# Two LayerNorms of a transformer block: half of the feature tiles turned by DMA instead of TensorE, and the stages behind them started with feature pairs by token halves

## The chip, the cores and the metric

The kernel runs on one core of a Trainium2 chip. Its engines are TensorE (PE; its weight loads have a row of their own, PEld), VectorE (DVE), ScalarE (ACT), GpSimd (POOL) and SyncE (SP, which issues nearly all DMAs). Each engine executes its own list of instructions in order, and engines wait for each other by semaphores. The metric is the device time of one execution in microseconds (us): 2433.39 us, the median of three runs (2433.3 to 2434.96).

## The reference

One layer of a streaming encoder on 256 tokens of 2048 features, all in float32:

```python
h = LN(alpha*h + 0.5*SwiGLU_1(h))                       # ffn1 and its LayerNorm
mix = W_out[ sig(g_A)*(A(h) W_oA) + sig(g_B)*(B(h) W_oB) ]
h = LN(alpha*h + mix)                                   # A: chunked attention, B: latent attention
h = LN(alpha*h + CrossAttn(h, LN(mem)))                 # cross attention and its LayerNorm
h = LN(alpha*h + 0.5*SwiGLU_2(h))                       # ffn2
# layer_norm(x, g, b): (x - mean) * rsqrt(var + eps) * g + b over the 2048 features
```

The change concerns the first and the third LayerNorm, and the products that come first behind each: the values of attention A (`h @ w_in`, 1024 of its columns) behind the first, and the first 512 gate and 512 up columns of ffn2 behind the third.

## The kernel before, in words

The stream `h` lies by tokens: two tiles `h0`, `h1` of 128 tokens x 2048 features (token halves, `tt` 0 and 1). A product needs it turned, features on the partitions: sixteen feature tiles `kt` of 128, four to a quarter, in blocks T0 to T3 (one block is one quarter, both token halves). Every operand is held as a high and a low part whose sum is the float32 value: ScalarE casts the high part, VectorE subtracts it for the low part. A product is then three matmuls: weight high with both parts of the stream, weight low with its high part. The stream is the stationary operand and 512 weight columns move.

**The two LayerNorms before the change.** The stage ahead ends with an output column whose products are computed for token half 0 first, then for half 1 (`skewed`, L813), from four weight pieces that are kept for both. So the statistics of half 0 are ready while TensorE works on half 1. `ln_steps` (L436) gives three steps for a half: `ln_scale` (mean and reciprocal root by a dozen small VectorE instructions), `ln_T` of quarters 0 and 1, and `ln_T` of quarters 2 and 3. `ln_T` (L406) scales a quarter (VectorE for even ones, L413; ScalarE for odd ones, L415), turns its four tiles on TensorE (L421), applies gain and bias from PSUM (two tiles on ScalarE, L428; two on VectorE, L430), and splits the result into its parts (L255, L256).

**The stages behind them before.** They are skewed too: four pieces of four feature tiles for half 0, 48 matmuls for all sixteen tiles and 512 columns, then the same four pieces for half 1, then four pieces of the next 512 columns for both halves. The steps of half 1's LayerNorm are woven in at 0, 3 and 4 items.

**Turning by DMA.** Elsewhere (the mixer's LayerNorm in `turned_norm`, L1386, the hidden units, the queries) a tile is turned without TensorE: ScalarE separates the two 16-bit halves of each float32 into planes (`planes`, L845/L846), SyncE issues a DMA that transposes 16-bit elements (`send`, L849/L850), and ScalarE joins the planes again (`join`, L852/L854). In `turned_norm` gain and bias follow (two tiles on ScalarE, L1426; two on VectorE, L1428), and the split.

**What sets the order.** `run` (L179) walks a list of items. It loads weight pieces ahead into three raw buffers (L193, 1 MB each), and splits them into two unit buffers `hi`/`lo` or into blocks that are free then. SyncE's list has the weight loads and the turning DMAs in one row; a load is put behind the last turning DMA (`issue_after(self.sent.ins)`, L192). Inside that, a tile scheduler orders the instructions of each engine once, when the program is built.

## Time and profile before

| | |
|---|---|
| median of three runs | 2433.39 us |
| profiled execution | 2432.52 us |
| its span, first to last instruction | 2430.7 us |
| PE busy | 2422.3 us (100%) |
| DVE busy | 2130.9 us (88%) |
| ACT busy | 1553.2 us (64%) |
| DMA, mean rate | 212 GB/s |
| chain that ended last | PE 89%, DVE 4%, ACT 3%, DMA 1% |

A busy engine executes an instruction; waiting doesn't count, but matmuls are pipelined and the end of one is modelled, so a short wait of TensorE can be hidden in its busy row. The row of its weight loads (PEld) is the sharper one: each matmul here has its own weight load, and their start times give TensorE's pace. The chain is followed back from the last instruction, at each step to what released it.

### The profile page before, as it was taken

Reading aid. Unit: us, or ns where it says so; the run is one execution under the profiler, and the core shown is the slowest. Engines: PE = TensorE matmul, PEld = TensorE weight load, DVE = VectorE, ACT = ScalarE, POOL = GpSimd, SP = SyncE. Lnnn points to the kernel's source line nnn. Section 1 sums busy time; section 2 is a strip of 40 time slices with the busy share of each in tenths; the row PEclk is TensorE's granted clock in tenths of the full one; section 3 lists DMA queues with packets and bytes.
Section 4 is the critical chain, followed back from the end, with each engine's and each line's share of the span. In section 5 each row is a group of like instructions: output and inputs, shape, how many; then the busy total and the mean of one; then the engine's idle time right before and its main releaser. Section 6 shows DMA issues by size and latency. Waiting matters only on the chain.

```text
span 2430.7 us, 29702 instructions
## 1 busy us (share of the span) xinstructions
PE 2422.3 (100%) x11280; PEld 2022.8 (83%) x11280; DVE 2130.9 (88%) x2437; ACT 1553.2 (64%) x2022; POOL 35.9 (1%) x81
## 2 busy tenths in 40 slices
PE   9999999999999999999999999999999999999999
PEld 8888888888888888888888888888888888888887
DVE  8999989899889998779788889979879999888997
ACT  6676745666555557878565687765666675556662
POOL 0000000000000001000000000000000000000000
PEclk9999999999999999999999999999999999999999
DMA  7766656667656657776577577655556766666665
GB/s 268 252 212 214 207 200 222 210 201 219 224 176 215 216 195 248 229 210 176 183 246 256 167 241 213 220 181 192 190 199 214 229 221 210 220 207 207 200 220 182
DMA packets 176414, 516.20 MB, mean 212 GB/s; under 512 B 111728, under 2 KB 112496, under 8 KB 121104
## 3 DMA queue, kind: packets, MB, share of 16 engines
q1 hardware_dynamic: 170816, 495.83, 61.6%
q0 software_dynamic: 4592, 17.30, 2.2%
q8 instruction: 88, 1.44, 0.2%
q10 hardware_dynamic: 864, 1.18, 0.1%
q14 instruction: 54, 0.44, 0.1%
HBM read 485.30 MB, written 2.10 MB: 201 GB/s over the span
## 4 chain that ended last, share of the span: by engine, by line
PE 89%; DVE 4%; ACT 3%; DMA 1%; issue 1%; SPq 0%; DVEq 0%; ACTq 0%
PE at L311 24%; PE mm L311 23%; PE at L366 11%; PE mm L366 11%; PE mm L298 10%; PE mm L277 4%; PE mm L279 2%; DVE lo L267 2%; ACT hi L264 1%; PE at L1034 1%; PE at L1505 0%; PE at L277 0%; DMA raw<-w_xv 0%; PE at L1088 0%; ACT H L854 0%
## 5 line engine op out<-in xcount | busy, mean ns | idle before, releaser
L264 ACT CAST hi<-raw 128x1024 fp32r<-128x1024 f32 (+1 forms) x852 | 804.0, 981 | 458.0 <-PE at L311 150.1
L267 DVE TENSOR_TENSOR lo<-raw,hi 128x2048 fp32r<-128x2048 f32 (+1 forms) x427 | 902.0, 2114 | 134.8 <-ACT hi L264 129.0
L311 PE MATMUL mm<-hi,T 128*128 128x512 f32 (+1 forms) x1312 | 307.5, 384 | 0.8 <-DVE v L400 0.7
L311 PEld LDWEIGHTS mm<-hi,T 128*128 128x128 f32 x1312 | 244.5, 188 | 46.9 <-DVE v L400 1.1
L264 ACT CAST X<-H 128x1024 fp32r<-128x1024 f32 (+1 forms) x170 | 174.8, 1035 | 160.9 <-DVE H L248 119.9
L311 PE MATMUL at<-hi,T 128*128 128x512 f32 x1136 | 272.3, 390 | 0.0
L311 PEld LDWEIGHTS at<-hi,T 128*128 128x128 f32 x1136 | 213.3, 188 | 44.5
L267 DVE TENSOR_TENSOR X<-H,X 128x2048 fp32r<-128x2048 f32 (+1 forms) x85 | 191.4, 2252 | 64.7 <-ACT X L264 64.7
L311 PE MATMUL mm<-lo,T 128*128 128x512 f32 (+1 forms) x656 | 158.4, 383 | 0.0
L311 PE MATMUL at<-lo,T 128*128 128x512 f32 x568 | 141.0, 389 | 0.0
L311 PEld LDWEIGHTS mm<-lo,T 128*128 128x128 f32 x656 | 122.3, 188 | 22.4
L311 PE MATMUL at<-hi,H 128*128 128x512 f32 x560 | 133.8, 390 | 0.0
L311 PEld LDWEIGHTS at<-lo,T 128*128 128x128 f32 x568 | 106.7, 188 | 22.1
L311 PEld LDWEIGHTS at<-hi,H 128*128 128x128 f32 x560 | 105.0, 188 | 21.5
L250 DVE TENSOR_TENSOR H<-H,raw 128x512 f32<-128x512 f32 (+1 forms) x170 | 115.4, 679 | 2.2
L311 PE MATMUL mm<-hi,H 128*128 128x512 f32 x480 | 115.5, 392 | 0.1
L311 PEld LDWEIGHTS mm<-hi,H 128*128 128x128 f32 x480 | 89.6, 188 | 18.9 <-DVE w L684 0.5
L248 DVE TENSOR_TENSOR H<-raw 128x1024 f32<-128x1024 f32 (+1 forms) x85 | 102.1, 1201 | 0.6 <-DMA raw<-w_gate 0.4
L366 PE MATMUL mm<-X,X 128*128 128x512 f32 x342 | 91.4, 393 | 0.0
L264 ACT CAST X<-raw 128x1024 fp32r<-128x1024 f32 (+1 forms) x54 | 55.4, 1035 | 47.9 <-DVE raw L250 38.6
L366 PE MATMUL at<-X,X 128*128 128x512 f32 (+1 forms) x315 | 82.6, 386 | 0.7 <-ACT X L264 0.7
L854 ACT COPY w<-w 128x1024 uint16<-128x1024 uint16 (+1 forms) x60 | 75.7, 1275 | 1.4 <-DMA w<-w 1.4
(387 smaller groups left out, 4151.3 us busy)
## 6 DMA issues: line engine op xcount, KB each, us to landing
raw<-ffn_w_in SPq DMA_DIRECT2D x150, 1024.0 KB, 4.9
raw<-ffn_w_out SPq DMA_DIRECT2D x66, 1024.0 KB, 4.9
raw<-w_gate SPq DMA_DIRECT2D x32, 1024.0 KB, 4.8
raw<-ffn_w_out_r SPq DMA_DIRECT2D x16, 1024.0 KB, 4.9
raw<-w_qk SPq DMA_DIRECT2D x16, 1024.0 KB, 5.6
raw<-w_o_b SPq DMA_DIRECT2D x16, 1024.0 KB, 4.8
raw<-w_out SPq DMA_DIRECT2D x16, 1024.0 KB, 5.0
raw<-w_xk SPq DMA_DIRECT2D x16, 1024.0 KB, 5.4
```

Of the source, the lines that this page charges most:

```text
L248: self.nc.vector.tensor_tensor(two[0], two[1], raw[:, :m].unsqueeze(1).to_broadcast([P, 2, m]), ALU.add)
L250: self.nc.vector.tensor_tensor(t[:, a * m:a * m + m], t[:, b * m:b * m + m], raw[:, a * m:a * m + m], ALU.add)
L264: self.last_hi = self.nc.scalar.copy(hi[:, c:d], src[:, c:d])
L267: self.last_lo = self.nc.vector.tensor_tensor(lo[:, :n], src, hi[:, :n].bitcast(F32), ALU.subtract)
L277: self.nc.tensor.matmul(ps, hi[j], x.both(kt), start=(j == 0), stop=False)
L279: self.last_mm = self.nc.tensor.matmul(ps[:, :S], lo[j], x.at(0, kt), start=False, stop=(j == n - 1))
L298: self.last_mm = self.nc.tensor.matmul(ps, x.at(xi, kt)[:, tt * P:(tt + 1) * P], w[wi][:, j * 512 + c:j * 512 + c + m], start=(start and j ...
L311: self.last_mm = self.nc.tensor.matmul(ps[tt, g][:, :n], x.at(xi, kt)[:, tt * P:(tt + 1) * P], w[wi][:, c:c + n], start=first and j + wi + ...
L366: self.last_mm = self.nc.tensor.matmul(bank[:, :m], a[xi], v[wi][:, c * m:(c + 1) * m], start=own and first and wi + xi == 0, stop=own and ...
L854: self.nc.scalar.copy(self.words(u, n).rearrange("p (c k) -> p k c", k=2), self.words(s, n).rearrange("p (k c) -> p k c", k=2))
L1034: nc.tensor.matmul(ps[:, c0:c0 + nk], q[:, tt * P:(tt + 1) * P], k[:, :nk], start=(j == 0), stop=(j == len(parts) - 1))
```

## The change

For the LayerNorms behind ffn1 and behind the cross attention, quarters 0 and 1 are still turned on TensorE (`near`, which calls `ln_T`). Quarters 2 and 3 take the way over DMA: `planes`, `send`, `join`, gain and bias, split, with blocks `F` and `X2` for the planes. All of quarters 2 and 3 is scaled on VectorE. These steps have priority 0, where the others keep the raised one.

The stage behind starts with `skewed_pairs`: a weight piece is now two feature tiles of two column groups (1024 columns). The first four pieces (feature tiles 0 to 7, quarters 0 and 1) run for token half 0, then again for half 1; the last four (tiles 8 to 15) for both halves at once. The number of matmuls and the bytes of weights are the same. Arrays of weights are laid out anew for that, before the kernel runs. Some PSUM tiles change banks (`n % 2 ^ 1` in the gates).

```diff
-                self.add(f, prio=prio, held=main[i][2] if i < len(main) else 0)
+                f, p = f if isinstance(f, tuple) else (f, prio)
+                self.add(f, prio=p, held=main[i][2] if i < len(main) else 0)
...
-    def mm_pair(self, ps, w, n, x, kts, first, last):
+    def mm_pair(self, ps, w, n, x, kts, first, last, tts=(0, 1)):
 
         for wi in range(2):
             for j, kt in enumerate(kts):
-                for tt in range(2):
+                for tt in tts:
...
-        first = self.collect(lambda: self.skewed(
-            part, (), (None, None, ("X0", "X1", "early"), ("H4", "H5"))))
-        self.weave(first, dict(zip((0, 3, 4), before)))
...
+        side = dict(before)
+        for i, c in enumerate(SUMS_IN):
+            side.setdefault(9 + i, []).append((self.forms_step(fx, SUMS_IN, c, xT), 0))
+        self.skewed_pairs(self.t[tag + "_w_in"][0], ps, xT, side, (None, None, ("X0", "X1", "early"), ("H4", "H5")))
...
+    def skewed_pairs(self, src, ps, xT, side, tags):
+
+        kept = {}
+
+        def add(k, tts, tags=None, held=0, keep=False, again=False):
+            def fn(w=None):
+                if keep:
+                    kept[k] = w
+                w = kept.pop(k) if again else w
+                if k == 0:
+                    ps.update({(tt, g): self.group_tile(0) for tt in tts for g in range(2)})
+                self.mm_pair(ps, w, 512, xT(), (2 * k, 2 * k + 1), k == 0, k == 7, tts)
+            self.add(fn, *(() if again else ((src[:, k * 2048:(k + 1) * 2048], tags),)), held=held)
+
+        def build():
+            self.skewed(lambda tt, k, **kw: add(k, (tt,), **kw), (), tags)
+            for k in range(4, 8):
+                add(k, (0, 1))
+        self.weave(self.collect(build), side)
...
+        va, ps, gates, fx = {}, {}, {}, {}
+
+        def values():
+            va["t"] = self.block("H4", (P, 2, 1024))
+            for n in range(2):
+                for tt in range(2):
+                    (nc.vector.tensor_copy if tt else nc.scalar.copy)(
+                        va["t"][:, tt, n * 512:(n + 1) * 512], ps[tt, n])
+        side = dict(steps(1))
+        for i, c in enumerate(SUMS_GATE):
+            side.setdefault(9 + i, []).append((self.forms_step(fx, SUMS_GATE, c, xT), 0))
+        side[12].insert(0, values)
+        self.skewed_pairs(t["w_va"][0], ps, xT, side, (None, None, ("H5", "H0", "early"), ("X0", "X1", "turned")))
...
-            self.pair_group(n % 2, t["w_gate"][n], 512, KT, xT, AT_GATE[n], fx, ps, qs, None, SUM_HOME + ("H5",),
+            self.pair_group(n % 2 ^ 1, t["w_gate"][n], 512, KT, xT, AT_GATE[n], fx, ps, qs, None, SUM_HOME + ("H5",),
...
-    def turned_norm(self, ln, st, x):
+    def turned_norm(self, ln, st, x, homes=("X2", "X3", "H5", "H4")):
...
+        def near(tt):
             def fn():
                 if tt == 0:
                     x["T"] = self.act(["T0", "T1", "T2", "T3"])
-                got[tt] = self.ln_scale(st[tt])
+                self.ln_T(self.h[tt], got[tt], tt, ln, x["T"], (0, 1))
...
+        if not homes[0]:
+            def low(f, *a):
+                return f(*a), 0
+            side = {0: [scale(1), low(send, 0, 2), low(planes, 0, 3)], 1: [low(send, 0, 3)], 2: [low(join, 0, 2)],
+                    3: [near(1)], 4: [low(join, 0, 3), low(planes, 1, 2)], 5: [low(send, 1, 2), low(planes, 1, 3)],
+                    6: [low(send, 1, 3)], 7: [low(join, 1, 2)], 8: [low(join, 1, 3)]}
+            return lambda tt: side if tt else ([scale(0)], [near(0)], [low(planes, 0, 2)])
...
-        ln = [self.ln_steps(n, st, x) for n in ("ln_ffn1", "ln_mix", "ln_x")]
+        ln = [self.turned_norm("ln_ffn1", st, x, (None, None, "F", "X2")), None, self.turned_norm("ln_x", st, x, (None, None, "F", "X2"))]
...
-    r["ffn2_gate"] = _tok(a["ffn2_w_in"][0][:, :512])
-    r["ffn2_up"] = _tok(a["ffn2_w_in"][0][:, D_FF:D_FF + 512])
...
-    r["w_va"] = _tok(w[:, 2 * aw:3 * aw])
+    r["w_va"] = _pairs(*_halves(w[:, 2 * aw:3 * aw]), 512, [()])
```

How this moves instructions is seen on ScalarE and SyncE. First ScalarE at the first of the two LayerNorms, before. `h_101` is token half 0, `at` is PSUM that TensorE's transposes fill, `w` holds a quarter with gain and bias, `T_768` and `T_769` are quarters 0 and 1 of the turned stream, `X_786` takes the fourth weight piece.

```order
L415 ACTIVATE h_101<-h_101,nb_5094,y_5091 128x512 x2
L428 ACTIVATE w_773_5150<-at_5145,vecs 128x128
L428 ACTIVATE w_775_5163<-at_5158,vecs 128x128
L428 ACTIVATE w_773_5150<-at_5145,vecs 128x128
L428 ACTIVATE w_775_5163<-at_5158,vecs 128x128
L255 CAST T_768_5140<-w_773_5150 128x4x128
L255 CAST T_769_5141<-w_775_5163 128x4x128
L264 CAST X_786_5224<-raw_5222 128x1024
```

The same place after. `F` and `X_782` hold the planes of quarters 2 and 3, `X_784` takes the fourth weight piece.

```order
L416 ACTIVATE h_101<-h_101,nb_5094,y_5091 128x512
L828 COPY F_5181<-h_101 128x1024
L429 ACTIVATE w_773_5150<-at_5145,vecs 128x128
L429 ACTIVATE w_775_5163<-at_5158,vecs 128x128
L429 ACTIVATE w_773_5150<-at_5145,vecs 128x128
L429 ACTIVATE w_775_5163<-at_5158,vecs 128x128
L828 COPY X_782_5200<-h_101 128x1024
L256 CAST T_768_5140<-w_773_5150 128x4x128
L256 CAST T_769_5141<-w_775_5163 128x4x128
L836 COPY F_5181<-F_5181 128x2x512
L1398 ACTIVATE F_5181<-F_5181,vecs 128x128 x2
L265 CAST X_784_5205<-raw_5203 128x1024 x2
```

Two copies into planes (L828) now stand among the activations, ahead of the casts into quarters 0 and 1, and one of the two scalings of `h_101` is gone; a join (L836) stands ahead of the casts of the fourth weight piece.

SyncE's list at the same place, before and then after. `raw_5222` and `raw_5203` are the fourth weight piece.

```order
L193 DMA raw_5047<-w_va 128x2048
L193 DMA raw_5222<-w_va 128x2048
L193 DMA raw_5345<-w_va 128x2048
L193 DMA raw_5364<-w_va 128x2048
L193 DMA raw_5422<-w_va 128x2048
```

```order
L194 DMA raw_5047<-w_va 128x2048
L832 DMA_TRANSPOSE F_5181<-F_5181 128x8x128
L194 DMA raw_5203<-w_va 128x2048
L832 DMA_TRANSPOSE X_782_5200<-X_782_5200 128x8x128
L194 DMA raw_5317<-w_va 128x2048
L832 DMA_TRANSPOSE F_5181<-F_5181 128x8x128
L194 DMA raw_5339<-w_va 128x2048
L832 DMA_TRANSPOSE X_782_5200<-X_782_5200 128x8x128
```

Each of the four turning DMAs stands ahead of a weight load: the fourth piece stands behind the first of them.

ScalarE at the second of the two LayerNorms, after. `F_14042` and `X_2167` hold the planes, `T_2153` and `T_2154` are quarters 0 and 1, `H_2169` takes the fourth weight piece.

```order
L416 ACTIVATE h_101<-h_101,nb_13951,y_13948 128x512
L828 COPY F_14042<-h_101 128x1024
L828 COPY X_2167_14061<-h_101 128x1024
L429 ACTIVATE w_2158_14008<-at_14003,vecs 128x128
L429 ACTIVATE w_2160_14021<-at_14016,vecs 128x128
L429 ACTIVATE w_2158_14008<-at_14003,vecs 128x128
L429 ACTIVATE w_2160_14021<-at_14016,vecs 128x128
L836 COPY F_14042<-F_14042 128x2x512
L256 CAST T_2153_13998<-w_2158_14008 128x4x128
L256 CAST T_2154_13999<-w_2160_14021 128x4x128
L1398 ACTIVATE F_14042<-F_14042,vecs 128x128 x2
L265 CAST H_2169_14066<-raw_14064 128x1024 x2
```

Here both copies into planes stand ahead of the activations, and the join of quarter 2 stands ahead of the casts into quarters 0 and 1.

## Rows read from the trace of the kernel before

**Rows 1.** The page: busy times, granted clock in 40 slices, one cast (mean ns).

```profile
PE 2422.3 (100%) x11280; PEld 2022.8 (83%) x11280; DVE 2130.9 (88%) x2437; ACT 1553.2 (64%) x2022; POOL 35.9 (1%) x81
...
PEclk9999999999999999999999999999999999999999
...
L264 ACT CAST X<-raw 128x1024 fp32r<-128x1024 f32 (+1 forms) x54 | 55.4, 1035 | 47.9 <-DVE raw L250 38.6
```

**Rows 2.** Waits of PEld: us in total, times, longest.

```profile
PEld mm L311 <- DVE v L400: 1.1, 1, 1.1
```

**Rows 3.** Windows: the stages behind both norms; us, busy (instructions) by engine, clock, DMA.

```profile
683.02:729.47 46.45, 46.45 (x218) 38.54 (x217) 40.15 (x73) 28.60 (x46) 1.23 (x2) 1.00 0.40 140
1741.09:1787.32 46.23, 46.23 (x218) 38.55 (x217) 34.67 (x63) 25.18 (x41) 0.00 (x0) 1.00 0.34 117
```

**Rows 4.** Timeline of PEld, first norm: start, us, instruction, idle before.

```profile
683.02 1.02 PEld L421 LDWEIGHTS at<-ident,h 128*128 128x128 f32 x8
...
684.43 1.45 PEld L298 LDWEIGHTS mm<-hi,T 128*128 128x128 f32 x7 [0.22 <-DVE T L256]
...
689.57 2.68 PEld L298 LDWEIGHTS mm<-H,T 128*128 128x128 f32 x12
692.29 1.03 PEld L421 LDWEIGHTS at<-ident,h 128*128 128x128 f32 x8
...
696.92 1.68 PEld L298 LDWEIGHTS mm<-hi,T 128*128 128x128 f32 x8
```

**Rows 5.** Timeline of PEld, second norm.

```profile
1741.09 1.02 PEld L421 LDWEIGHTS at<-ident,h 128*128 128x128 f32 x8
...
1754.78 1.68 PEld L298 LDWEIGHTS mm<-hi,T 128*128 128x128 f32 x8
```

**Rows 6.** Timeline of ACT, first norm, token half 0.

```profile
679.75 1.52 ACT L415 ACTIVATE h<-h,nb,y 128x512 f32<-128x512 f32 x2 [4.88 <-DVE nb L403]
681.17 1.73 ACT L428 ACTIVATE w<-at,vecs 128x128 f32<-128x128 f32 x4
683.03 1.14 ACT L255 CAST T<-w 128x512 fp32r<-128x512 f32 x2
```

**Rows 7.** Timeline of ACT, second norm, token half 0.

```profile
1740.20 1.14 ACT L255 CAST T<-w 128x512 fp32r<-128x512 f32 x2
```

**Rows 8.** Timeline of DVE, both norms: scalings, a low part, weights' low part.

```profile
683.68 0.69 DVE L256 TENSOR_TENSOR T<-w,T 128x512 fp32r<-128x512 f32 x1 [0.34 <-ACT T L255]
...
691.43 2.29 DVE L267 TENSOR_TENSOR X<-raw,X 128x2048 fp32r<-128x2048 f32 x1
...
1736.26 1.00 DVE L413 TENSOR_SCALAR h<-h,mv,y 128x512 f32<-128x512 f32 x2
```

**Rows 9.** Lines of the DMA way elsewhere: ns min/median/max, first and last start.

```profile
L846 ACT COPY X<-h x4: 1038/1044/1046, 1383.9 to 1390.7; 128x1024 uint16<-128x1024 uint16 x4
...
L854 ACT COPY X<-X x4: 1361/1368/1384, 1388.3 to 1407.6; 128x1024 uint16<-128x1024 uint16 x4
...
L1426 ACT ACTIVATE X<-X,vecs x8: 480/504/517, 1389.7 to 1412.9; 128x128 f32<-128x128 f32 x8
...
L1428 DVE TENSOR_SCALAR X<-X,vecs x8: 340/341/347, 1390.1 to 1410.3; 128x128 f32<-128x128 f32 x8
```

**Rows 10.** Timeline of SP: weight loads at the first norm; a turning DMA elsewhere.

```profile
666.11 8.02 SPq L193 DMA_DIRECT2D raw<-w_va  x3
...
1400.31 1.23 SPq L850 DMA_TRANSPOSE H<-H  x1
```

**Rows 11.** DMAs near 1401.5 (spaced) and 1391.3 (crowded): KB, us to landing.

```profile
raw<-w_xk SPq DMA_DIRECT2D x1, 1024.0 KB, 5.6
H<-H SPq DMA_TRANSPOSE x1, 3.1
...
raw<-w_xk SPq DMA_DIRECT2D x1, 1024.0 KB, 7.3
X<-X SPq DMA_TRANSPOSE x1, 6.1
```

More of the change, by code (lines that the diff above doesn't have):

```diff
@@ L434, in ln_T @@
                 self.ln_act = turned
-    def ln_steps(self, ln, st, x):
-        def steps(tt):
-            e = {}
-            def scale():
-                e["mr"] = self.ln_scale(st[tt])
-            def quarters(qs):
-                def fn():
-                    if tt == 0 and qs[0] == 0:
-                        x["T"] = self.act(["T0", "T1", "T2", "T3"])
-                    self.ln_T(self.h[tt], e["mr"], tt, ln, x["T"], qs)
-                return fn
-            return [scale], [quarters((0, 1))], [quarters((2, 3))]
-        return steps
     def gb_apply(self, i, h, qs=range(4)):
@@ L873, in mixer @@
         e = self.__dict__
-        va, kept, ps1 = {}, {}, {}
-        def val(n, tts, g, ps, tags=None, held=0, keep=False, again=False):
-            def fn(w=None):
-                if keep:
-                    kept[g] = w
-                w = kept.pop(g) if again else w
-                for tt in tts:
-                    if g == 0:
-                        ps[tt] = self.mm_tile()
-                    self.mm_tok(ps[tt], tt, w, xT(), range(4 * g, 4 * g + 4), g == 0, g == 3)
-                if g == 3:
-                    if "t" not in va:
-                        va["t"] = self.block("H4", (P, 2, 1024))
-                    for tt in tts:
-                        (nc.vector.tensor_copy if tt else nc.scalar.copy)(
-                            va["t"][:, tt, n * 512:(n + 1) * 512], ps[tt])
-            ap = t["w_va"][n, :, g * 2048:(g + 1) * 2048]
-            self.add(fn, *(() if again else ((ap, tags),)), held=held)
-        ps = {}
-        first = self.collect(lambda: self.skewed(
-            lambda tt, g, **kw: val(0, (tt,), g, ps, **kw), (),
-            (None, None, ("H5", "H0", "early"), ("X0", "X1", "turned"))))
-        a, b, c = steps(1)
-        self.weave(first, {0: a, 3: b, 4: c})
-        gates, fx = {}, {}
-        second = self.collect(lambda: [val(1, (0, 1), g, ps1) for g in range(4)])
-        self.weave(second, {1 + i: [self.forms_step(fx, SUMS_GATE, c, xT)] for i, c in enumerate(SUMS_GATE)}, prio=0)
+        va, ps, gates, fx = {}, {}, {}, {}
[10 more added lines that the diff above has]
+        self.skewed_pairs(t["w_va"][0], ps, xT, side, (None, None, ("H5", "H0", "early"), ("X0", "X1", "turned")))
         bias = {}
@@ L981, in lat_join @@
             return fn
-        self.pair_group(0, t["w_lat"][0], 512, KT, xT, SUMS_IN, fx, lps, lqs, None, SUM_HOME + ("H5",))
+        self.pair_group(1, t["w_lat"][0], 512, KT, xT, SUMS_IN, fx, lps, lqs, None, SUM_HOME + ("H5",))
         self.add(lat_scale, prio=SOON)
@@ L996, in kpe @@
             rope = self.rotation()
-            ps = self.at_tile()
+            ps = self.mm_tile()
             for kt in range(KT):
@@ L1393, in fn @@
             def fn():
+                if tt == 0 and homes[0]:
+                    x["T"] = self.act(["T0", "T1", "T2", "T3"])
+                got[tt] = self.ln_scale(st[tt])
+            return fn
+        def near(tt):
+            def fn():
                 if tt == 0:
                     x["T"] = self.act(["T0", "T1", "T2", "T3"])
-                got[tt] = self.ln_scale(st[tt])
+                self.ln_T(self.h[tt], got[tt], tt, ln, x["T"], (0, 1))
             return fn
@@ L1401, in fn @@
                 if tt == 0:
-                    e[q] = self.block(("X2", "X3", "H5", "H4")[q], (P, 2, 2, 512))
+                    e[q] = self.block(homes[q], (P, 2, 2, 512))
                 mean, r, nb = got[tt]
@@ L1710, in _layout @@
         r[f + "_w_in"] = _pairs(
-            w[:, D_FF:D_FF + NG * 512], w[:, :NG * 512], 512, [AT_FIRST] + [SUMS_IN] * (NG - 1))
+            w[:, D_FF:D_FF + NG * 512], w[:, :NG * 512], 512, [AT_FIRST if f == "ffn1" else ()] + [SUMS_IN] * (NG - 1))
         r[f + "_w_in_r"] = _pairs(
```

21 lines of the change are left out of this document (removed).

## The prediction

> **What bounds the kernel.** I read the page first, then TensorE's waits, the two stages in windows, and the timelines of each engine there. On the page TensorE is busy for 100% of the span at the full granted clock (2.4 GHz of its two levels) [rows 1]. The list of waits agrees: the longest single wait of its weight loads is 1.1 us, in another stage [rows 2]. So a microsecond taken from TensorE's list is gained, and a microsecond that it newly waits is lost; other engines matter only where TensorE waits for them. The two stages behind the norms take 46.45 and 46.23 us [rows 3]. Twelve matmuls take 2.72 us, from 689.57 to 692.29 [rows 4], 0.2267 each. A stage holds 192 of them, 43.5 us; what is left in the second window, 2.7 us, is 24 transposes, so 0.9 us per eight. The first window has 0.2 us more, a short wait for the low part of the turned stream at 684.43 [rows 4].
>
> **What is removed.** Each norm gives up sixteen of its 32 transposes: 4 x 0.9 = 3.6 us over both, and the 0.2 us wait. If nothing new is waited for, that is all there is to gain: 3.8 us, 0.16%.
>
> **What comes instead.** For each half, ScalarE gets two copies into planes (1.04 us each) and two joins (1.36) [rows 9] for one scaling less; VectorE gets one scaling more. Both have idle time over the whole kernel [rows 1], but here their place in the list counts. In a row of ScalarE's the next instruction starts some 0.09 us before the end of the one ahead, so I count a copy as 0.95. I follow the chain to the first matmuls of each half.
>
> *First norm, half 0.* Before, ScalarE's two scalings ran from 679.75 in 1.52 us, four activations followed, and the cast into T0 began at 683.03 [rows 6]. Now one scaling (0.72) is gone and two copies (1.9) stand ahead of that cast, 1.2 us more: cast from 684.2 to 684.8, low part 0.69 later [rows 8], 685.5. TensorE comes there at 683.02, where eight transposes were [rows 4]. Its first two matmuls use high parts, the third needs the low one, so it runs as if it had started at 685.05: 2.0 us lost.
>
> *First norm, half 1.* The fourth weight piece is now behind a turning DMA on SyncE. Before, it was loaded far ahead: three more loads of the stage go out between 666.11 and 674.1 [rows 10]. Now the first copy ends at 681.7, the turning DMA takes SyncE 1.23 us [rows 10], and the load goes at 683.0. A load behind one turning DMA landed in 5.6 us [rows 11], so 688.7. ScalarE's next instruction but for a short idle is its cast, and everything for half 1 is queued behind: two casts of the piece to 690.7 (1.04 each [rows 1]), the scaling of h1 691.4, cast of T2 692.0, join 693.3, two activations with gain and bias (0.49 each) 694.1, a wait of 0.2 for VectorE and the cast of T3 694.9, the copy of half 1 into planes 695.8, four activations 697.3, cast into T0 698.1; low part 698.8. VectorE has 2.29 us of the piece's low part [rows 8] in that time and keeps up. TensorE's own way: 685.05 + 36 matmuls 8.16 + eight transposes 0.9 + 12 matmuls 2.72 = 696.85. It needs the low part for the second matmul, so it runs as if from 698.6: 1.75 us lost. Before, this second half began at 696.92 [rows 4]: with the transposes saved up to there, the stage is 1.7 us behind.
>
> *Second norm, half 0.* VectorE scales quarters 0 and 2 from 1736.26 to 1737.26 [rows 8]; the copy of quarter 2 ends at 1738.4, that of quarter 3 at 1739.3, the activations at 1740.8. Then the join of quarter 2 stands ahead of the cast into T0, and waits for the turning DMA: 1738.4 + 3.1 [rows 11] = 1741.5, joined 1742.9, cast to 1743.5 (before, the cast began at 1740.20 [rows 7]). VectorE has a column with gain and bias (0.34 [rows 9]) and an addition to h1 (0.68) ahead of the low part: 1744.5. TensorE comes at 1741.09 [rows 5] and runs as if from 1744.05: 3.0 us lost.
>
> *Second norm, half 1.* The fourth piece is issued at 1739.65 and lands at 1745.25. Queued behind: two casts 1747.3, cast of T2 1747.9, join 1749.2, two activations 1750.0, scaling 1750.7; then ScalarE waits for VectorE, which subtracts the piece's low part until 1752.3 and applies gain and bias; cast of T3 1753.2, copy 1754.2, activations and a short wait 1755.85, cast into T0 1756.5, low part 1757.2. TensorE comes at 1744.05 + 11.8 = 1755.85 and runs as if from 1757.0: 1.1 us lost. Before, this half began at 1754.78 [rows 5], so 2.2 us behind.
>
> *Quarter 2 of half 1*, needed 52 matmuls after the start of that half, 12.0 us to the first that reads its low part. ScalarE's chain from the same start: 1.85 until the first piece's high buffer is free, two casts 1.95, copy 0.95, two casts 1.95, two joins 2.6, three activations 1.2, a cast 0.6, then the low part 0.7, in all 11.8. I count no wait, but there is no slack: a late DMA here shows in full.
>
> *The rest.* Later weight pieces are needed 5.4 us apart and cost ScalarE 2 and VectorE 2.3 of that; the changed PSUM banks keep the same number of tiles. I count them at nothing; a bound is the longest wait found now, 1.1 us, per stage.
>
> **The sum.** -3.6 - 0.2 + 2.0 + 1.75 + 3.0 + 1.1 = +4.05 us; by the starts of the second halves, 1.7 + 2.2 = 3.9. I take +4.0: 2436.5 for an execution like the profiled one (2432.52, of it 1.8 outside the span). The median of the runs lies 0.9 above that execution, so 2437.4, 0.17% slower.
>
> **Rival 1: the gain stays.** The items come in time, and the change is worth its 3.8 us: 2429.6. For it: the waits are sums of a dozen durations, and VectorE's and ScalarE's shares leave room. Against it: copies and joins stand ahead of the casts in lists that run in order, so 2.0 and 3.0 do not depend on a DMA being a little faster. Nor does a faster one help much at the second norm: half 1 is tied to the weight load, and what half 0 wins, half 1 waits.
>
> **Rival 2: loads and turning DMAs delay each other.** Where they were crowded, a turning DMA took 6.1 us and a load 7.3 [rows 11]. At 6.1 the second norm's half 0 starts 3.0 us later, and quarter 2 of half 1 comes about 3 us late at both places; the load's 1.7 us adds to half 1 at the first. In all some 9 us more, +13: 2446. It decides from a turning DMA of about 4 us, where the loss passes 0.2%. Against it: the first turning DMA of each half here goes out with no load issued in the 4 us before it, as in the spaced case.
>
> **Rival 3: the clock falls.** The row shows the full level in every slice, but no wait as long as the 3.0 us that I count [rows 1, 2]. If the clock went to its lower level (1.2 GHz) there, a matmul of 0.227 would take twice that, and 36 matmuls until the next transposes would cost 8 us: 2445. The Trainium skill (TensorE: Matmul & The Clock Gate, "Why this matters for your kernels") warns of idle gaps between bursts of matmuls, after which the clock goes back to half; by that rule the sum would be about +12, by the row alone +4. No run here shows it.
>
> **How the numbers follow.** A measurement of this kernel can tell about 0.2% (4.9 us) from no change. The chain as worked out, with a microsecond or two of error on each of five links, +1.5 to +7: 0.50, of it 0.33 within 0.2% and 0.17 slower. Rival 1 and what lies between it and +1.5: 0.25, of it 0.03 faster by more than 0.2%, since 3.8 us is not enough for that. Rival 2: 0.17. Rival 3: 0.08. So faster 0.03, same 0.55, slower 0.42. The range goes from the full gain, 2430, to most of rival 2, 2444; the forecast's own is 2435 to 2440.
>
> **What would show it.** In the profile after: TensorE waits of 2 to 3 us ahead of the first matmuls of half 0 at both norms, put down to ScalarE or VectorE, and of 1 to 2 us ahead of half 1; the second halves beginning 1.5 to 2.5 us later than 696.92 and 1754.78; the fourth piece's load landing near 688.7 and 1745.3; turning DMAs of 3 to 4 us. Wrong would be first matmuls without a wait (rival 1), turning DMAs of 6 us (rival 2), a granted clock under 1.00 (rival 3), or a loss that lies in another stage.

## The result and the profile after

The changed kernel takes 2439.06 us (median of 12 runs, 2437.86 to 2443.81) against 2434.44 us for the kernel before beside it (12 runs, 2432.79 to 2438.05). The ratio is 1.0022 with a 95% interval of 1.0014 to 1.0029, which is 3.4 to 7.1 us slower. In a second comparison, with other runs of both, it is 1.0024 (1.0015 to 1.0034). The forecast was 0.17% slower and 2437.4 us; of the 1.7 us between, 1.05 lie in the runs of before, which here have a median that much above the one shown earlier.

The profiled execution takes 2437.89 us, its span 2436.1. The page, with the lines that answer to [rows 1]: engine busy times and the granted clock.

```profile
PE 2422.5 (99%) x11248; PEld 2018.6 (83%) x11248; DVE 2132.0 (88%) x2441; ACT 1567.4 (64%) x2034; POOL 35.9 (1%) x81
...
PEclk9999999999999999999999999999999999999999
```

TensorE has 32 instructions less (the transposes), but is no longer busy for all of the span. The list of its waits says where, and answers to [rows 2], where 1.1 us was the longest (total us, times, longest):

```profile
PEld mm L312 <- ACT T L256: 5.0, 4, 1.9
...
PEld mm L312 <- DVE T L257: 2.4, 4, 0.8
```

Line 256 is the cast into T and line 257 its low part (255 and 256 before; from line 175 to 435 the numbers are one higher, so 421 is now 422; further on 846 is 828, 850 is 832, 854 is 836). The matmuls of the two stages were line 298 and are line 312 now, that of `mm_pair`. Four waits of each kind, 7.4 us: one pair ahead of each half at each norm. The windows of the two stages, from TensorE's arrival to the next stage, answer to [rows 3]:

```profile
682.76:731.65 48.89, 47.03 (x202) 37.77 (x200) 40.78 (x74) 35.67 (x53) 1.23 (x2) 0.97 0.69 221
1744.82:1792.90 48.08, 45.66 (x202) 36.52 (x200) 35.95 (x65) 31.87 (x47) 0.00 (x0) 1.00 0.61 197
```

Each has 16 TensorE instructions less, 202 for 218, and is longer, by 2.44 and 1.85 us: 4.3 together. The other 1.1 us of the two spans' distance of 5.4 lies outside of them, where nothing was changed; between the two stages alone, two traces of before differ by 2.5 us (below, 9). The timeline of TensorE's weight loads behind the first norm, in place of [rows 4]:

```profile
684.63 0.30 PEld L312 LDWEIGHTS mm<-hi,T 128*128 128x128 f32 x2 [1.88 <-ACT T L256]
685.54 2.14 PEld L312 LDWEIGHTS mm<-hi,T 128*128 128x128 f32 x6 [0.61 <-DVE T L257]
687.78 1.48 PEld L312 LDWEIGHTS mm<-lo,T 128*128 128x128 f32 x4
...
698.56 0.19 PEld L312 LDWEIGHTS mm<-hi,T 128*128 128x128 f32 x1 [0.20 <-ACT T L256]
```

And behind the second norm, in place of [rows 5]:

```profile
1746.51 0.30 PEld L312 LDWEIGHTS mm<-hi,T 128*128 128x128 f32 x2 [1.72 <-ACT T L256]
1747.61 1.24 PEld L312 LDWEIGHTS mm<-hi,T 128*128 128x128 f32 x6 [0.81 <-DVE T L257]
...
1760.04 0.30 PEld L312 LDWEIGHTS mm<-hi,T 128*128 128x128 f32 x2 [1.17 <-ACT T L256]
1760.77 1.23 PEld L312 LDWEIGHTS mm<-hi,T 128*128 128x128 f32 x6 [0.43 <-DVE T L257]
```

What ScalarE does at the first norm (it answers to [rows 6]; the copies into planes are L828, the joins L836):

```profile
680.44 1.05 ACT L828 COPY F<-h 128x1024 uint16<-128x1024 uint16 x1
681.39 1.75 ACT L429 ACTIVATE w<-at,vecs 128x128 f32<-128x128 f32 x4
683.03 1.03 ACT L828 COPY X<-h 128x1024 uint16<-128x1024 uint16 x1
683.97 1.14 ACT L256 CAST T<-w 128x512 fp32r<-128x512 f32 x2
...
689.01 2.00 ACT L265 CAST X<-raw 128x1024 fp32r<-128x1024 f32 x2 [1.75 <-DMA raw<-w_va]
```

The cast into T began at 683.03 before; now the second copy begins there, and the cast 0.94 us later. The last line is the other half of the story: the fourth weight piece, for which ScalarE idles 1.75 us. SyncE's queue and the landings of the two DMAs issued from 683.45 to 685.4 (KB, us from issue to landing) say why:

```profile
681.51 1.87 SPq L832 DMA_TRANSPOSE F<-F  x1
683.48 0.53 SPq L194 DMA_DIRECT2D raw<-w_va  x1
```

```profile
raw<-w_va SPq DMA_DIRECT2D x1, 1024.0 KB, 5.5
X<-X SPq DMA_TRANSPOSE x1, 5.9
```

The load stands behind the turning DMA, goes at 683.48 and lands at 689.0. Before, it was issued by 674.1 [rows 10].

### The profile page after: what moved, and what is told of

Its sections match the earlier page's. It is cut to its first block, busy times and chain, and to the rows that moved or that the text cites. A ratio compares the mean times of both kernels' runs of the same rounds, so it can differ in the third digit from the quotient of the medians.

```text
span 2436.1 us, 29676 instructions
## 1 busy us (share of the span) xinstructions
PE 2422.5 (99%) x11248; PEld 2018.6 (83%) x11248; DVE 2132.0 (88%) x2441; ACT 1567.4 (64%) x2034; POOL 35.9 (1%) x81
## 3 DMA queue, kind: packets, MB, share of 16 engines
q8 instruction: 88, 1.44, 0.2%
## 4 chain that ended last, share of the span: by engine, by line
PE 90%; DVE 3%; ACT 3%; DMA 2%; issue 1%; SPq 0%; DVEq 0%; ACTq 0%
PE mm L312 27%; PE at L312 25%; PE at L367 11%; PE mm L367 11%; PE mm L299 5%; PE mm L278 4%; PE mm L280 2%; DVE lo L268 1%; PE at L999 1%; ACT hi L265 1%; PE at L278 1%; DMA raw<-w_va 1%; PE at L1484 0%; DMA raw<-w_o_b 0%; PE at L1053 0%
## 5 line engine op out<-in xcount | busy, mean ns | idle before, releaser
L312 PE MATMUL mm<-hi,T 128*128 128x512 f32 (+1 forms) x1424 | 337.4, 386 | 5.3 <-ACT T L256 3.5
L312 PEld LDWEIGHTS mm<-hi,T 128*128 128x128 f32 x1424 | 265.7, 189 | 58.6 <-ACT T L256 5.0
L312 PE MATMUL at<-hi,T 128*128 128x512 f32 x1216 | 291.3, 389 | 0.0
L312 PEld LDWEIGHTS at<-hi,T 128*128 128x128 f32 x1216 | 228.2, 188 | 47.8
L312 PE MATMUL mm<-lo,T 128*128 128x512 f32 (+1 forms) x712 | 173.9, 384 | 0.0
L312 PEld LDWEIGHTS mm<-lo,T 128*128 128x128 f32 x712 | 133.2, 188 | 25.0
L312 PE MATMUL at<-lo,T 128*128 128x512 f32 x608 | 150.3, 389 | 0.0
L312 PEld LDWEIGHTS at<-lo,T 128*128 128x128 f32 x608 | 114.1, 188 | 23.7
L367 PEld LDWEIGHTS mm<-X,X 128*128 128x128 f32 x360 | 66.8, 188 | 16.0 <-DVE X L268 2.2
```

The lines of the kernel that those rows point to most:

```text
L312: self.last_mm = self.nc.tensor.matmul(ps[tt, g][:, :n], x.at(xi, kt)[:, tt * P:(tt + 1) * P], w[wi][:, c:c + n], start=first and j + wi + ...
L367: self.last_mm = self.nc.tensor.matmul(bank[:, :m], a[xi], v[wi][:, c * m:(c + 1) * m], start=own and first and wi + xi == 0, stop=own and ...
```

## The experiments

The theory: TensorE waits for ScalarE's list, which runs in order and has copies and joins ahead of the casts (half 0), and for the fourth piece, whose load stands behind a turning DMA (half 1). All variants were timed beside the kernel before. The stages are from one trace each, measured from TensorE's arrival as above; "sum" is their sum less 92.68 us (before, [rows 3]).

| kernel | stage 1, 2 (us) | sum | ratio to before (95%) |
|---|---|---|---|
| before, second trace | 46.22, 46.24 | -0.2 | |
| changed, three traces | 48.89, 48.08; 48.51, 48.11; 48.95, 48.41 | +4.3, +3.9, +4.7 | 1.0022 (1.0014 to 1.0029), 1.0024 (1.0015 to 1.0034) |
| 1 turned on TensorE | 46.47, 46.24 | 0.0 | 0.9999 (0.9991 to 1.0008) |
| 2 loads ahead | 46.88, 47.61 | +1.8 | 1.0015 (1.0006 to 1.0023) |
| 3 copies behind | 49.51, 49.02 | +5.9 | 1.0028 (1.0019 to 1.0037) |
| 4 = 2 and 3 | 46.25, 46.18 | -0.2 | 1.0008 (0.9999 to 1.0017) |
| 5 = 4, GpSimd for half 0 | 47.09, 46.81 | +1.2 | 1.0015 (1.0007 to 1.0024) |
| 6 = 4, a join later | 46.43, 46.05 | -0.2 | 1.0006 (0.9997 to 1.0015) |
| 7 = 6, that join later still | 46.58, 46.47 | +0.4 | 1.0007 (0.9998 to 1.0016) |
| 8 = 7, sixth piece's casts later | 45.28, 44.88; 45.37, 44.90 | -2.5, -2.4 | 0.9992 (0.9983 to 1.0001), 0.9994 (0.9986 to 1.0003) |

**1. All quarters turned on TensorE, pairs kept.**

```diff
-            side = {0: [scale(1), low(send, 0, 2), low(planes, 0, 3)], 1: [low(send, 0, 3)], 2: [low(join, 0, 2)],
...
+            def far(tt):
+                return lambda: self.ln_T(self.h[tt], got[tt], tt, ln, x["T"], (2, 3))
+            side = {0: [scale(1)], 3: [near(1)], 4: [far(1)]}
```

> The changed kernel with all four quarters of both norms turned on TensorE again; the tile pairs by token halves stay. Theory (the loss is TensorE waiting for ScalarE's list, which the copies and joins lengthen, and for the fourth weight piece, whose load stands behind a turning DMA): the waits ahead of both halves go (under 0.4 us each), the transposes come back (0.9 us per eight), both stages take 46 to 47 us, ratio to before 0.9995 to 1.0008 (2433 to 2436.5 us). Rival (the order by tile pairs, the new packing or the moved PSUM banks cost the time): the stages stay near 48 to 49 us, ratio 1.0015 to 1.003.

The time is that of before, and the windows have 218 TensorE instructions again:

```profile
683.72:730.19 46.47, 46.47 (x218) 38.52 (x217) 40.16 (x72) 28.58 (x45) 1.23 (x2) 1.00 0.40 146
1742.91:1789.15 46.24, 46.24 (x218) 38.53 (x217) 35.46 (x64) 24.05 (x39) 0.00 (x0) 1.00 0.34 125
```

So the order by pairs, the packing and the PSUM banks cost nothing that can be seen; the loss is in how half of the tiles are turned.

**2. The loads ahead of the turning DMAs.** The fourth and fifth piece of each stage are requested before the first half's transposes.

```diff
-        done, highs = 0, []
+        done, highs, self.prefetch = 0, [], lambda k: [fetch(i) for i in range(nxt, min(nxt + k, len(queue)))]
...
-                    x["T"] = self.act(["T0", "T1", "T2", "T3"])
+                    x["T"] = self.prefetch(2) and self.act(["T0", "T1", "T2", "T3"])
```

> The changed kernel with the fourth and fifth weight piece of each stage loaded ahead of the first turning DMA. Theory: the waits ahead of half 1 (0.2 + 0.5 us and 1.2 + 0.4 us) go, since the fourth piece's casts no longer hold up ScalarE's list; the waits ahead of half 0 (1.9 + 0.6 and 1.7 + 0.8 us) stay. About 2.3 us less than the changed kernel: 2436 to 2437.5 us, ratio to before 1.0007 to 1.0015. Rival (loads and turning DMAs delay each other): the turning DMA takes 5 to 6 us beside the loads, half 0's joins come later, nothing is gained: 1.002 or more. Rival (half 1 is late by ScalarE's own work, the load is not on the chain): same as the changed kernel, 1.0022.

As the theory has it: the waits ahead of half 0 stay (1.87 + 0.61 and 1.89 + 0.81 us), those ahead of half 1 fall to 0.34 and 0.93, and the stages get 2.5 us shorter. With the loads out of the way the turning DMAs of half 0 all take 3.0 to 3.2 us; in the changed kernel those of quarter 3, beside loads, took 5.9 and 7.8. Of half 1's wait at the second norm 0.93 us is left with no load in the chain. It is VectorE's list: there ScalarE twice idles for it, while VectorE works from 1742.80 to 1752.79 without a gap and has the low part of a weight piece (2.28 us) ahead of the scaling that the copy into planes needs:

```profile
1749.26 0.82 ACT L416 ACTIVATE h<-h,nb,y 128x512 f32<-128x512 f32 x1 [1.64 <-DVE nb L404]
1752.37 1.05 ACT L828 COPY F<-h 128x1024 uint16<-128x1024 uint16 x1 [2.30 <-DVE h L1377]
```

**3. The copies behind the casts.**

```diff
-                with self.tc.issue_after(self.next_hi.ins):
+                with self.tc.issue_after((self.next_hi if homes[0] else self.ln_act).ins):
                     self.planes(hs, e[q][:, tt, 0, :], 512)
```

> The changed kernel with the copies into planes issued behind the cast of each half's second quarter, not ahead of it; the loads as in the changed kernel. Theory: the waits ahead of half 0 shrink from 2.5 us to under 1 us at both norms, but the turning DMA and with it the fourth piece's load go 2 to 3 us later, so that half 1 waits 2 to 4 us instead: time within 1.5 us of the changed kernel, ratio to before 1.0015 to 1.003. Rival (each wait is on its own, and what half 0 wins is kept): 4 to 5 us less than the changed kernel, 0.9995 to 1.0005.

Half 0 hardly waits now, at the first norm and at the second:

```profile
683.11 0.30 PEld L312 LDWEIGHTS mm<-hi,T 128*128 128x128 f32 x2 [0.52 <-ACT T L256]
...
1748.42 1.46 PEld L312 LDWEIGHTS mm<-hi,T 128*128 128x128 f32 x7 [0.33 <-DVE T L257]
```

The piece's load goes at 685.88 in place of 683.48, and TensorE waits for the piece itself, then for half 1's casts:

```profile
696.06 0.77 PEld L312 LDWEIGHTS mm<-X,T 128*128 128x128 f32 x4 [1.57 <-DVE X L268]
698.02 0.50 PEld L312 LDWEIGHTS mm<-hi,T 128*128 128x128 f32 x2 [1.19 <-ACT T L256]
```

What half 0 wins is lost at half 1: the waits are not each on their own, half 1 is tied to the load. The stages are longer than those of the changed kernel by another 1.2 to 1.9 us, and the clock can account for that. Behind the waits of half 1 the granted clock is at 0.50 for some 3 us at both norms (window, us, busy by engine, clock, DMA):

```profile
699.00:700.00 1.00, 1.00 (x4) 0.80 (x4) 1.00 (x3) 1.00 (x3) 0.00 (x0) 0.50 0.00 0
...
1764.00:1765.00 1.00, 1.00 (x4) 0.81 (x3) 0.99 (x2) 1.00 (x2) 0.00 (x0) 0.50 0.06 16
```

Ten matmuls take 3.4 us there at the first norm and 3.5 at the second, in place of 2.27: 2.4 us in all. Whether the fifth pair would have waited more at the full clock isn't known.

**4. Both edits.**

> Both edits together: loads of the fourth and fifth piece ahead of the turning DMAs, copies into planes behind the casts. Theory: nothing long is left of the four waits (0.5 us each at most), and half of the transposes are gone: 2431.5 to 2433.5 us, ratio to before 0.9987 to 0.9997. Rival (what is won ahead of half 1 is lost at quarter 2 of half 1, whose planes are now copied later): a wait of 1 to 3 us ahead of the fifth pair of tiles, 1.0 or more. Rival (loads and turning DMAs delay each other): 1.001 or more.

The stages are those of before. The expected gain of 0.7 us or more did not come: half 0 waits 0.9 and 0.3 us, but half 1 still 1.5 and 1.75. In ScalarE's list the join of quarter 3 of half 0, with its activations and cast, stands ahead of half 1's casts, and is not needed before the seventh pair: the next candidate. The rival, that quarter 2 would be late, was wrong here: no wait at the fifth pair.

**5. Half 0's copies and joins on GpSimd.** Experiment 4 with `nc.gpsimd.tensor_copy` in place of `nc.scalar.copy` for half 0.

> The kernel with both edits, and the copies into planes and the joins of half 0 on GpSimd in place of ScalarE (half 1's stay on ScalarE). If ScalarE's list is the cause, the waits ahead of half 1 shrink from 1.5 and 1.75 us to under 0.5 us, and the stages to about 45 us each, ratio 0.9985 to 0.9995. Rival (GpSimd is slow at this: one of its operations on 128x512 elements took 1.27 us in the trace, so a copy of the double count of halved words may take 2.5 us and more, and ScalarE's activations on half 0's quarters stand ahead of half 1's scaling and wait for it): a wait of 3 us or more ahead of half 1 at one norm or both, ratio 1.001 or more.

GpSimd is not slow at it, 1.04 to 1.29 us a copy and 1.34 to 1.79 a join, and ScalarE's busy time in the first stage falls from 36.41 to 32.46 us. Yet half 1 waits 2.0 us at the first norm and 2.1 at the second. The expectation failed, though its rival's reason, a slow GpSimd, was wrong too. ScalarE's list is less full and waits more: its activations and casts of half 0's quarters 2 and 3 stand ahead of the scaling of h1 and idle there, 1.93 and 0.85 us for VectorE at the first norm and 1.44 and 0.82 us for the joins at the second. The last wait ahead of half 1's casts is for VectorE at both norms, 1.59 + 0.32 and 1.83 us for its gain and bias:

```profile
695.16 0.46 ACT L429 ACTIVATE w<-at,vecs 128x128 f32<-128x128 f32 x1 [1.59 <-DVE w L431]
...
1757.18 0.80 ACT L429 ACTIVATE w<-at,vecs 128x128 f32<-128x128 f32 x2 [1.83 <-DVE w L431]
```

VectorE had become later, and part of it is that some of its operations took longer while GpSimd copied: an operation with gain and bias 1.40 us (0.28 to 0.35 otherwise), a low part into T 1.20 (0.69), two of them 2.38 (1.29).

```profile
686.79 1.34 POOL L836 COPY X<-X 128x1024 uint16<-128x1024 uint16 x1 [1.41 <-DMA X<-X]
...
686.81 1.40 DVE L1400 TENSOR_SCALAR F<-F,vecs 128x128 f32<-128x128 f32 x1
```

So this run does not say what a ScalarE with less work is worth by itself.

**6. Experiment 4, with the join of quarter 3 of half 0 behind half 1's casts.**

```diff
-                    3: [near(1)], 4: [low(join, 0, 3), low(planes, 1, 2)], 5: [low(send, 1, 2), low(planes, 1, 3)],
-                    6: [low(send, 1, 3)], 7: [low(join, 1, 2)], 8: [low(join, 1, 3)]}
+                    3: [near(1)], 4: [low(planes, 1, 2)], 5: [low(send, 1, 2), low(planes, 1, 3)],
+                    6: [low(send, 1, 3)], 7: [low(join, 1, 2)], 8: [low(join, 0, 3), low(join, 1, 3)]}
```

> The kernel with both edits (loads ahead, copies behind the casts), and the join of quarter 3 of half 0, with its activations and cast, moved from ahead of half 1's casts to behind the joins of quarter 2 of half 1. Theory (what is left of the waits ahead of half 1, 1.5 and 1.75 us, is ScalarE's list once more, and this join is not needed before the seventh pair of tiles): these waits shrink to under 0.5 us, the stages take 45.0 to 45.3 us each (before 46.45 and 46.23), ratio to before 0.9985 to 0.9995. Rival (the work moved is in the way of quarter 2 or 3 of half 1, which then come late): a wait of 1 to 3 us ahead of the fifth or the seventh pair, stages of 46 us or more, 0.9998 or more.

Here the rival came true, by its wait. Half 1 waits 0.34 and 0.31 us, but the fifth pair, which needs quarter 2 of half 1, now waits at both norms:

```profile
712.44 2.36 PEld L312 LDWEIGHTS mm<-hi,T 128*128 128x128 f32 x11 [1.39 <-DVE T L257]
...
1772.60 2.37 PEld L312 LDWEIGHTS mm<-hi,T 128*128 128x128 f32 x11 [1.24 <-DVE T L257]
```

(In this trace TensorE also waited 2.79 us ahead of the first stage, for a scaling that an earlier weight load had delayed. That hides half 0's wait there, and the clock, low behind it, is at 0.75 on average from 686 to 689, inside the stage. So its 46.43 us is no clean measure; experiment 7, without this, has the same wait at the fifth pair.)

**7. The join of experiment 6 one step later still,** behind the cast of quarter 2 of half 1.

```diff
-                self.join(v[:, 1, :], v[:, 0, :], 512)
+                self.join(v[:, 1, :], v[:, 0, :], 512, e.get("done") if (tt, q) == (0, 3) else None)
...
-                self.split(a, *(x["T"].blk(s, 4 * q, 4)[:, :, tt * P:(tt + 1) * P] for s in (0, 1)))
+                e["done"] = self.split(a, *(x["T"].blk(s, 4 * q, 4)[:, :, tt * P:(tt + 1) * P] for s in (0, 1)))
```

> The kernel before this one (join of quarter 3 of half 0 behind half 1's casts), with that join put one step later still: behind the cast of quarter 2 of half 1, so that it no longer stands between that quarter's join (1.36 us) and its cast. Theory: the wait of 1.39 and 1.24 us ahead of the fifth pair of tiles falls under 0.4 us, no other comes in its place, and the stages, 46.43 and 46.05 us in the kernel before this one (46.45 and 46.23 before the change), take 44.6 to 45.2 us each. Ratio to before 0.9983 to 0.9997 (2430 to 2433 us). Rival (the list is simply full, and the next piece's casts or quarter 3 are late in turn): a wait of 1 us or more ahead of the fifth or the seventh pair, stages of 45.7 us or more, ratio 1.0000 or more.

The wait stayed, 1.36 and 1.70 us. The join was not what made quarter 2 late. ScalarE at the first norm in this kernel:

```profile
701.65 0.88 ACT L1398 ACTIVATE F<-F,vecs 128x128 f32<-128x128 f32 x2
704.46 2.00 ACT L265 CAST hi<-raw 128x1024 fp32r<-128x1024 f32 x2 [1.93 <-DMA raw<-w_va]
706.36 0.62 ACT L256 CAST T<-F 128x512 fp32r<-128x512 f32 x1
```

Quarter 2's cast (the last line) could have gone after its activations; instead the casts of the sixth weight piece stand ahead of it, and wait 1.93 us for their load.

**8. The sixth piece's casts behind quarter 2's cast.** The join of quarter 2 is handed to the scheduler two items earlier, so that the casts of the next weight piece can be tied to its cast. `self.hold` is set to what the split of quarter 2 of half 1 returns, and the casts of the next piece are issued after it.

```diff
-                first = {"turned": self.ln_act, "next": self.last_hi}.get(tags[2]) if tags and len(tags) > 2 else None
+                first = {"turned": self.ln_act, "next": self.last_hi}.get(tags[2]) if tags and len(tags) > 2 else self.hold
...
-                    got = self.halves(raw[:, :ap.shape[1]], hi, lo)
+                    got, self.hold = self.halves(raw[:, :ap.shape[1]], hi, lo), None
...
-                    3: [near(1)], 4: [low(planes, 1, 2)], 5: [low(send, 1, 2), low(planes, 1, 3)],
-                    6: [low(send, 1, 3)], 7: [low(join, 1, 2)], 8: [low(join, 0, 3), low(join, 1, 3)]}
+                    3: [near(1)], 4: [low(planes, 1, 2)], 5: [low(send, 1, 2), low(planes, 1, 3), low(join, 1, 2)],
+                    6: [low(send, 1, 3)], 8: [low(join, 0, 3), low(join, 1, 3)]}
```

> The kernel before this one, with the casts of the sixth weight piece put behind the cast of quarter 2 of half 1 on ScalarE. In the kernel before this one ScalarE idled 1.93 and 1.79 us for that piece's load and spent 2.0 us on its casts while quarter 2's activations were done. Theory: the wait of 1.36 and 1.70 us ahead of the fifth pair goes to under 0.4 us, the stages take 44.8 to 45.4 us each (before the change 46.45 and 46.23), ratio to before 0.9984 to 0.9998. Rival (the sixth piece's casts are then late themselves): a wait of 1 us or more ahead of the sixth pair, stages of 45.8 us or more, ratio 1.0000 or more.

```profile
701.43 0.88 ACT L1398 ACTIVATE F<-F,vecs 128x128 f32<-128x128 f32 x2
703.03 0.62 ACT L256 CAST T<-F 128x512 fp32r<-128x512 f32 x1 [0.73 <-DVE F L1400]
704.25 2.00 ACT L265 CAST hi<-raw 128x1024 fp32r<-128x1024 f32 x2 [0.60 <-DMA raw<-w_va]
```

Now nothing waits at the fifth pair, nor at the sixth, and the stages are 45.28 and 44.88 us long:

```profile
683.23:728.51 45.28, 45.21 (x202) 36.63 (x201) 40.24 (x73) 36.60 (x52) 1.24 (x2) 1.00 0.60 189
1744.58:1789.46 44.88, 44.88 (x202) 36.71 (x201) 35.78 (x64) 31.58 (x46) 0.00 (x0) 1.00 0.55 175
```

That is 2.5 us under before, of the 3.8 that the transposes are worth; what is left are waits of 0.9 us ahead of half 0 at the first norm and 0.3 elsewhere. Whether the join has to be moved for this, and what this edit does without the others, was not tried. Since its interval still reached 1, it was run again:

> The kernel before the last (sixth piece's casts behind quarter 2's cast) once more, since its interval still reached 1. If its two stages, 45.28 and 44.88 us in the trace (46.45 and 46.23 before the change), are all that differs, the time is 2.5 us under before: ratio 0.9984 to 0.9997. If not, it was chance, and the ratio is 0.9997 to 1.0005.

It gave 0.9994 (0.9986 to 1.0003) and stages of 45.37 and 44.90. Neither interval alone excludes 1. Taken as independent, the two together give about 0.9993, with a half width of 0.0009/1.41 = 0.0006, so 0.9987 to 0.9999. Against the changed kernel in the same runs it is 0.9994/1.0024 = 0.9970 by the two ratios, 7 us.

**9. The changed kernel twice more, and before once more.**

> The changed kernel once more, to see what repeats. Expected to repeat: the four waits ahead of the halves, 7.4 us in all within 1 us, and the two stages at 48 to 49 us. Expected not to repeat, if it was chance: the granted clock of 0.50 for 3 us at the first norm. If the clock follows from the wait, it falls there again.

> The changed kernel beside it on the same chip, for the distance between the two. By the stages of the traces (48.89 + 48.08 us and 48.51 + 48.11 us against 45.28 + 44.88) it is 6.5 us slower than the kernel with all the edits, and 4 us slower than before: ratio to before 1.0012 to 1.0025.

The waits repeat in their places, 0.2 us more than the expectation allows: 8.6 us in the first of these traces (1.59 + 0.65, 1.70 + 0.54, 1.74 + 0.81, 1.15 + 0.43), with stages of 48.5 and 48.1 us. The ratio of the second is in the range expected of it. The low clock at the first norm did not repeat; the second of these traces has one at the second norm (below).

> The kernel before the change once more, for a second trace. In the traces of the variants TensorE waits 0.6 to 3.5 us for one weight piece of the cross attention stage near 1400 us, where nothing is changed; in the trace of before it waits 0.5. If that wait is chance, it can be anything from 0.5 to 3.5 us here, and the two changed stages take 46.2 to 46.5 us as before; if the variants cause it, it is 0.5 us again.

The wait near 1400 us was 0.43 us here, 0.70 in experiment 1, and from 0.62 to 3.46 in the eleven traces of kernels that turn by DMA, four times under 0.8 and six times over 1.5. Three traces without it are too few to say that it makes the long wait more likely, though none of them has one. It does show how much chance there is in one trace: between the two stages the two traces of before differ by 2.5 us (1011.62 and 1014.16).

## Why the prediction was right, step by step

**The gain.** 3.6 us by 32 transposes: right. Experiment 1 puts them back, and the stages return to 46.47 and 46.24. The 0.2 us wait counted with them is not a constant; the second trace of before does not have it.

**First norm, half 0 (2.0 us).** The low part was forecast for 685.5, and the load that needs it began at 685.54. By the forecast's reckoning (two matmuls ahead of it, 685.09 as the start) the loss is 2.3 us, since TensorE came 0.26 us earlier.

**First norm, half 1 (1.75 us).** The chain was right link by link, each within 0.5 us: load at 683.0 (683.48), landed 688.7 (689.0), the four activations over at 697.3 (697.76), the low part at 698.8 (the matmul that reads it loads its weights at 699.28). In the first trace the wait is only 0.74 us, for a reason that the forecast did not have: TensorE came 1.5 us late, after a stretch at the lower clock. In the two other traces it is 2.2 and 2.5 us. Experiment 2 takes the load off the chain, and the wait falls to 0.3.

**Second norm, half 0 (3.0 us).** Too large by 0.5 us: waits of 2.5 in all three traces, 2.3 by the reckoning used above. The turning DMA took the 3.1 us counted, but VectorE's scaling, with which the chain begins, started 5.4 us ahead of TensorE's arrival, where the trace of before has 4.8 [rows 5, 8].

**Second norm, half 1 (1.1 us).** Under-sized by 0.5 us: 1.6 us in the first two traces. The load was late as forecast, issued at 1742.85 and landed in 5.8 us (5.6 counted); without it, in experiment 2, 0.93 us stays, for VectorE. This error and the one before are the same: the low part of half 1 came 16.0 us after TensorE's arrival (16.1 in the forecast), and half 0 had taken 0.6 us less of that time, so TensorE waited the more. The two terms together are 4.1 us in the forecast and 4.1 in the first trace, so that they cancel is no luck. (The third trace has no wait here; its half 0 ran into the low clock.)

**Quarter 2 of half 1 (no wait, no slack).** Right on both counts. The changed kernel does not wait there, and its low part is done at 711.03 and 1772.28, where TensorE's sixth matmul of the fifth pair, the first to read it, comes at 711.0 and 1772.3. Experiments 6 and 7, in which ScalarE's order ahead of it changed, wait 1.2 to 1.7 us.

**The rest at nothing.** Right by experiment 1 for packing and banks; and in the changed kernel's trace nothing waits at the later pieces.

**The sum (+4.05 us).** +4.3, +3.9 and +4.7 us by the stages. The timed difference, 4.6 us by the medians and 5.4 by the ratio, is above it, and so is that of all variants that turn by DMA, by 0.6 to 2.4 us. The intervals cover that, but for experiment 5 and, at its edge, 4. By its own line of 0.2% the forecast held "same" for likelier than "slower", 0.55 to 0.42; the ratio of 1.0022 is just past that line.

Much of the excess goes with the clock. The record has the mean granted clock of every timed run to three digits; one fall of some 3 us makes it 0.999 (the first trace of the changed kernel), three make it 0.998 (experiment 3's). It is under 1.000 in 65 of the 111 runs of kernels that turn by DMA here, in 1 of the 11 of experiment 1 and in 1 of the 105 of before beside the variants. In experiments 4, 6, 7 and the first timing of 8, the runs at 1.000 differ from before by +0.4, +0.1, +0.1 and -3.4 us (medians), within 0.9 us of the sums of the stages (-0.2, -0.2, +0.4, -2.5), and the other runs take 3.1 to 4.2 us more. Experiment 5 fits less well (+2.6 against +1.2), experiments 2 and 3 have a single run at 1.000, and the changed kernel shows 1.1 us between the two groups in the first comparison and nothing in the second. A fall comes with the wait ahead of it, and these figures, sorted after the fact, do not part the two. Where the clock fell in a run without a trace isn't known; in the traces it did at or just ahead of the two norms, and in three of them near 1400 us, behind that stage's long wait (experiments 3 and 8, the changed kernel's third). Why the kernels that turn by DMA have it so often stays open.

**Rival 1, the gain stays:** wrong for this order of the work. Its counterargument, that what half 0 wins half 1 waits, is experiment 3. Experiment 8 shows that the gain was there to be had, two thirds of it, by edits of order alone, as the stages show it; the time shows it only with both timings taken together.

**Rival 2, loads and turning DMAs delay each other:** it was to decide from a turning DMA of 4 us. The first of each half took 3.0 to 3.2 us, like the spaced one [rows 11]. Those of quarter 3 of half 0 did take 5.9 and 7.8 us beside loads, as the rival has it, but had a half's time in hand.

**Rival 3, the clock falls:** it did fall, after a wait shorter than the 3.0 us counted, and not in every execution; in the traced stages of the changed kernel it cost next to nothing. In the first trace of the changed kernel the granted clock after the wait reads (window, us, busy by engine, clock, DMA):

```profile
685.00:686.00 1.00, 0.82 (x3) 0.43 (x2) 1.00 (x3) 1.00 (x2) 0.00 (x0) 0.82 0.47 131
686.00:689.00 3.00, 3.00 (x8) 2.34 (x7) 2.67 (x13) 1.23 (x3) 0.00 (x0) 0.50 1.01 321
689.00:690.00 1.00, 1.00 (x6) 0.77 (x5) 0.25 (x1) 0.99 (x2) 0.00 (x0) 0.97 1.24 358
```

0.50 is the lower level, 1.2 GHz; the waits ahead of it were 1.88 and 0.61 us, with two matmuls between. From 685.54 to 689.31 TensorE loads weights for ten matmuls, 3.77 us in place of 2.27: 1.5 us lost. The forecast of this rival took the slow stretch to last for 36 matmuls and 8 us; it lasted 3 us. And it was hidden: half 1 could not start before its cast at 697.88 in any case, so that TensorE waited that much less there: the stage is 48.89 us long, and 48.51 and 48.95 in the traces in which the clock stayed up at this norm. That it was hidden is luck of the place: in experiment 3 the clock fell behind half 1's wait, which could then hide nothing, and ten matmuls at each norm took 2.4 us more together; and in most variants a lower clock goes with a longer time (the sum, above). The prediction had the fall as a rival of 8 us more with a chance of 0.08; here it is a frequent event of 1 to 1.6 us.

## What to carry to other kernels

Where an engine works through its list in order, first ask what stands ahead of the one instruction that the bounding engine waits for, not how busy the engine is: taking 4 us of work off ScalarE in each stage did not help (VectorE's list was then late), and putting two casts behind another, with a join handed over two items earlier, gained 2.9 us. A queue that carries both loads and transfers that wait for an engine makes the loads wait too, so issue the loads first. Edits of order are tied to each other: the loads ahead gained 2.5 us by themselves, the copies behind the casts only moved the wait on, and the step under the time of before came with the last edit on top of the others.

## What the runs showed of the hardware that was not expected

**The clock after a wait is not decided by the wait's length in the trace.** The first norm's waits were 1.88 + 0.61 us where the clock fell to 0.50, and 1.87 + 0.61 in experiment 2 and 1.85 + 0.61 in the third trace of the changed kernel, where it stayed at 1.00. That third trace has it at the second norm instead, after 1.75 + 0.81 us:

```profile
1750.00:1751.00 1.00, 0.83 (x2) 0.71 (x3) 1.00 (x3) 0.32 (x1) 0.00 (x0) 0.67 1.15 198
1751.00:1752.00 1.00, 1.00 (x4) 0.75 (x3) 0.93 (x6) 0.79 (x1) 0.00 (x0) 0.50 1.44 381
```

The second trace of the changed kernel has it nowhere in these stages. Near 1400 us it fell after a wait of 3.40 us in experiment 8 and stayed at 1.00 after one of 3.46 in experiment 4. So a wait of 2.5 to 3.5 us here sometimes costs 1 to 1.6 us more, and sometimes not. Experiment 8 has a mean clock under 1.000 in 6 of 11 runs of its first timing and in 1 of 11 of its second.

**One weight load in an untouched stage lands very differently from run to run.** For the same piece of w_xk near 1400 us, issued between turning DMAs on SyncE, TensorE waited 0.43 and 0.49 us in the two traces of before, and 0.6 to 3.5 in those of the variants. A single profile's span is therefore not a measure of an edit of 2 us; the windows of the edited stages are, where the clock stays up in them.

**VectorE can be slower while GpSimd copies.** In experiment 5 three of VectorE's groups took 1.7 to 4 times as long beside a GpSimd copy or join as without (above); over the first stage VectorE is busy for 42.0 us, against 40.9 in experiment 4. Others, an addition to h1 at 684.07 among them, kept their 0.68 us.
